# Expert gates scattered into DRAM, and expert products with 512-column records, in a float32 hybrid block kernel

## The chip, the cores and the metric

The program runs on one core of one Trainium2 chip. The metric is the device time of one execution in microseconds (us), as the median of several runs. A profiled execution gives the trace from which all rows below come.

## What is computed

The block takes 256 tokens of width 2048. After adaptive norms, a gated delta net and sparse attention, it ends with a layer of 128 x 128 = 16,384 experts (PEER), and this is the part that is changed:

```python
def tok_block(i):
    xb = lax.dynamic_slice_in_dim(ht, i * TB, TB, axis=0)              # 128 tokens
    qh = (xb @ wq).reshape(TB, PEER_HEADS, PEER_QDIM)                  # 8 heads
    s1 = jnp.einsum('thd,hkd->thk', qh[..., :half], keys1)             # 128 scores
    s2 = jnp.einsum('thd,hkd->thk', qh[..., half:], keys2)
    v1, i1 = lax.top_k(s1, 16)
    v2, i2 = lax.top_k(s2, 16)
    cand = (v1[..., :, None] + v2[..., None, :]).reshape(TB, PEER_HEADS, 256)
    cidx = (i1[..., :, None] * 128 + i2[..., None, :]).reshape(TB, PEER_HEADS, 256)
    sc, pos = lax.top_k(cand, 16)
    eidx = jnp.take_along_axis(cidx, pos, axis=-1)                     # 8 x 16 experts of a token
    gw = jax.nn.softmax(sc, axis=-1)
    act = jax.nn.gelu(jnp.einsum('td,thkd->thk', xb, u[eidx]))
    return jnp.einsum('thk,thkd->td', gw * act, v[eidx])
```

Each token has 128 gates (8 heads of 16 experts). The kernel does not gather `u` and `v` by token: it computes gelu(u x) of all experts for all tokens, multiplies by a matrix of gates that is zero where an expert was not chosen, and multiplies by all of `v`.

## The kernel before, in words

All products are made in float32 by splitting each operand into a high part of a reduced float32 (`whi`, `hi`) and the rest (`wlo`, `lo`). A product is three matmuls: high x high, high x low, low x high. `Stream` (line 446) loads the weights in pieces by SP into `raw` (4 tiles of 128 x 1024), and for each 512 columns ACT casts `whi` and DVE subtracts `wlo`; 4 such pairs are open at a time. Line 289 is the helper through which every instruction is recorded, so the trace names it for nearly all, and instructions are told apart by their tiles.

Small work runs as generators in `Background` (line 316): after each step of the main loop `bg.step()` lets each of up to 8 open tasks run to its next `yield`, whose value is the planner's time at which it goes on. The planner's times (`Times`, line 196) only set the order of the instructions, which is fixed when the program is built.

The stages that the change touches:
- **The block's first stages** (until about 1040 us): norm, projections, delta net, attention. After the first projection the tasks `pre_task` and others are put in. ACT casts, activates, and issues a few DMAs here.
- **Query stage**: `wq` makes the 16 half-queries; `route_task` follows behind on DVE: scores, top 16 of each half, top 16 of the sums, for each of the 8 heads. After the last head it works out, in pieces of 1024 columns, the indices `i` and `j` of each chosen expert and the softmax, transposes these to put tokens on columns, and splits the gates into three bf16 parts (`gs`).
- **u loop** (line 1875 on): 128 steps j; step j makes the products of expert group (all i, this j) with all 256 tokens, 16 k-tiles of 3 matmuls of 256 columns (`stat256`), then a gelu into column block j of the matrix `A` (`act_by`).
- **`gate_task`** (line 1854) runs beside the u loop, 64 times for 4 tokens each: DVE builds one-hot matrices `oi` (128 x 128 x 4) and `ow` (three gate parts x one-hot), PE multiplies them (12 bf16 matmuls of 128 columns) into a gate matrix of 128 i x 128 j per token, DVE multiplies that into the columns of `A` that exist already, and ACT copies it to those that do not.
- **v loop** (line 2020 on): two halves of 1024 output columns, each 128 steps j: `w_split(j)` splits `A` of step j into `wh` and `wl`, and 12 matmuls of 512 columns follow. In the first half `g2_task` runs beside it: 64 DVE products with `ada_t`, whose loads SP issues. At its end POOL (GpSimd) issues the loads for the last norm.

POOL issues DMAs of its own queue in order, SP those of the weights.

Of the kernel before, what the change touches and what calls it, by code (L numbers as in the profile page):

```python
# [18 lines left out]
T = 256  # L19
# [48 lines left out]
def _const_array():  # L68
# [13 lines left out]
    add("one", np.ones(128))  # L82
    add("ones", np.ones((128, 128)))
# [96 lines left out]
NPAIR = 3  # L180
WO = [(512 * j, 512) for j in range(4)]
# [224 lines left out]
def _build(nc, tc, A, out, stacks, dump, at, stop_at):  # L406
# [33 lines left out]
    bg = Background(times, 8, lambda: "first" in done and next(ada_gen, None), lambda: PACE2 if "o7" in done else PACE)  # L440
# [108 lines left out]
    crowd = dram.tile([1, D], F32, name="crowd")  # L549

# [1115 lines left out]
    h2h = [hp.tile([128, 4, T], F32R, name="ht") for _ in range(4)]  # L1666
    h2l = [hp.tile([128, 4, T], F32R, name="ht") for _ in range(4)]
# [15 lines left out]
    for k in range(17):  # L1683
        if k == 0:
            stream.advance(0)
        if k < 16:
            pk = pairs[k // 2][:, k % 2 * 256:k % 2 * 256 + 256]
            hi, lo = h2h[k // 4][:, k % 4, :], h2l[k // 4][:, k % 4, :]
            h32 = xp.tile([128, T], F32, name="h32b", bufs=2)
            act(hi, pk, AF.Identity, bias=mcol[:, 3, k:k + 1], scale=mcol[:, 4, k:k + 1])  # L1690
            V.tensor_scalar(h32, pk, mcol[:, 4, k:k + 1], mcol[:, 3, k:k + 1], op0=OP.mult, op1=OP.add)
            V.tensor_tensor(lo, h32, hi, OP.subtract)
            if k % 2 == 0 and len(pairs) < 8:
                pairs += h2_pairs([len(pairs)])
        if k:
            h, l = stream.get()
            hi, lo = h2h[(k - 1) // 4][:, (k - 1) % 4, :], h2l[(k - 1) // 4][:, (k - 1) % 4, :]
# [5 lines left out]
    for k in range(4):  # L1703
        dump(f"h2h{k}", h2h[k])
        dump(f"h2l{k}", h2l[k])
# [5 lines left out]
    sp = pool(st_A, "sp", side=RIGHT)  # L1711
    st_e = stack()
# [23 lines left out]
    eqs = [qs_[:, 1024 * i:1024 * i + 1024] for i in range(2)]  # L1736
# [9 lines left out]
    gate = tmp(256)  # L1746
    eidx = tmp(512).rearrange("p (w b n) -> p w b n", w=2, b=2)

    ij = [ep.tile([128, T], BF, name=f"ij{n}") for n in range(2)]
    gs = [ep.tile([128, T], BF, name=f"gs{n}") for n in range(3)]  # L1750
    iota4 = ep.tile([128, 128, 4], BF, name="iota4")
    V.tensor_copy(iota4, C("iota")[:, :, None].to_broadcast([128, 128, 4]))
# [9 lines left out]
    def route_task():  # L1762
# [24 lines left out]
        V.tensor_copy(iif, ii)  # L1787
        V.tensor_scalar(au, posu, 4, None, op0=OP.logical_shift_right)
        V.tensor_copy(af[:, 0], au)
        V.tensor_scalar(au, posu, 15, None, op0=OP.bitwise_and)  # L1790
        V.tensor_copy(af[:, 1], au)
        yield bg.now() + RPACE
        for tb in range(2):
            for w in range(2):
                for h0 in (0, 4):
                    hs_ = slice(h0, h0 + 4)
                    eq = eqs[w].rearrange("p (h s k) -> p h s k", h=4, s=16)
                    V.tensor_tensor(eq, af[:, w, tb, hs_, :, None].to_broadcast([128, 4, 16, 16]),
                                    C("iota")[:, None, None, 0:16].to_broadcast([128, 4, 16, 16]), OP.is_equal)
                    yield bg.now() + RPACE  # L1800
                    V.tensor_tensor(eq, eq, iif[:, tb, w, hs_, None, :].to_broadcast([128, 4, 16, 16]), OP.mult)
                    yield bg.now() + RPACE
                    V.tensor_reduce(eidx[:, w, tb, :].rearrange("p (h s) -> p h s", h=8)[:, hs_], eq, axis=AX.X,
                                    op=OP.add)
                    yield bg.now() + RPACE
        for tb in range(2):
            V.tensor_tensor(gw[:, tb], scv[:, tb], scv[:, tb, :, 0:1].to_broadcast([128, 8, 16]), OP.subtract)
        yield bg.now() + RPACE
        act(gw, gw, AF.Exp)
        yield bg.now() + RPACE  # L1810
        sm = vv[:, 0, 0, :, 0:2].rearrange("p h b -> p b h")
        V.tensor_reduce(sm, gw, axis=AX.X, op=OP.add)
        V.reciprocal(sm, sm)
        V.tensor_tensor(gw, gw, sm[:, :, :, None].to_broadcast([128, 2, 8, 16]), OP.mult)
        yield bg.now() + RPACE
        for dst, src in zip((*ij, gate), (eidx[:, 0], eidx[:, 1], gw.rearrange("p b h s -> p b (h s)"))):
            S.copy(dst, transpose_to(ps(), src, 2).rearrange("p b t -> p (b t)"))
            yield bg.now() + RPACE
        for n in range(3):
            V.tensor_copy(gs[n], gate)  # L1820
            if n < 2:
                V.tensor_tensor(gate, gate, gs[n], OP.subtract)
        done.add("gate")

    def stat256(p, h, l, k0, n):

        for k in range(n):
            kk = k0 + k
            w, wl_ = h[:, k * 128:(k + 1) * 128], l[:, k * 128:(k + 1) * 128]
            a, b = h2h[kk // 4][:, kk % 4, :], h2l[kk // 4][:, kk % 4, :]  # L1830
# [19 lines left out]


    j_there, t_there = 0, 0

    def gate_task():
        nonlocal t_there
        nt = 4
        yield from wait_for("gate")
        ones, sums = {}, {}
        start, steps = bg.now(), 0
        pace = ((128 - j_there) * 5.15 - GEND) / (4 * T / nt)  # L1860

        def pause():
            nonlocal steps
            steps += 1
            return start + steps * pace

        def make(t0):
            oi = ep.tile([128, 128, nt], BF, name="oi", bufs=2)
            ow = ep.tile([128, 3, 128, nt], BF, name="ow", bufs=2)
            over = lambda a: a[:, None, t0:t0 + nt].to_broadcast([128, 128, nt])  # L1870
            V.tensor_tensor(ow[:, 2], iota4, over(ij[1]), OP.is_equal)
            V.tensor_tensor(oi, iota4, over(ij[0]), OP.is_equal)
            yield -pause()
            for n in range(3):
                V.tensor_tensor(ow[:, n], ow[:, 2], over(gs[n]), OP.mult)
            ones[t0] = oi, ow

        def products(t0):
            oi, ow = ones.pop(t0)
            p = ps()  # L1880
            for t in range(nt):
                for n in range(3):
                    PE.matmul(p[:, 128 * t:128 * t + 128], oi[:, :, t], ow[:, n, :, t], start=n == 0, stop=n == 2)
            sums[t0] = p

        def put(t0):
            nonlocal t_there
            pv = sums.pop(t0).rearrange("p (t j) -> p j t", t=nt)
            for q, (a, b) in enumerate(((0, JA), (JA, 128))):
                m = min(max(j_there, a), b)  # L1890
                x = act_by[q][:, :, t0:t0 + nt]
                if m > a:
                    V.tensor_tensor(x[:, :m - a], x[:, :m - a], pv[:, a:m], OP.mult)
                if m < b:
                    S.copy(x[:, m - a:], pv[:, m:b])
            t_there = t0 + nt

        yield from make(0)
        yield pause()
        for t0 in range(0, T, nt):  # L1900
            if t0 + nt < T:
                yield from make(t0 + nt)
                yield -pause()
            if t0:
                put(t0 - nt)
            yield pause()
            products(t0)
            yield pause()
        put(T - nt)
        done.add("gates")  # L1910

    bg.add(gate_task())
    for j in range(128):
        if j == JA:
            need("gate")
        p = ps()
        for i in range(4):
            h, l = stream.get()
            stat256(p[:, :T], h, l, 4 * i, 4)
        a = at_j(j)  # L1920
        n = t_there
        if n:
            t = ep.tile([128, T], F32, name="aj", bufs=2)
            act(t[:, :n], p[:, :n], AF.Gelu_apprx_tanh)
            V.tensor_tensor(a[:, :n], a[:, :n], t[:, :n], OP.mult)
        if n < T:
            act(a[:, n:], p[:, n:T], AF.Gelu_apprx_tanh)
        j_there = j + 1
    need("gates")
# [5 lines left out]
    vp_ = lambda: hp.tile([128, 1024], F32, name="ht")  # L1935
    ssf = sp.tile([128, 2, 4], F32, name="ssf")
# [10 lines left out]
    def g2_task():  # L1947
# [16 lines left out]
    bg.add(g2_task())  # L1964

# [59 lines left out]
    V.memset(ssf, 0.0)  # L2025
    ws = [w_split(j) for j in range(AHEAD)]
# [49 lines left out]
```

## Time and profile before

| | us |
|---|---|
| median of 3 runs (lowest to highest) | 2703.28 (2698.82 to 2706.44) |
| the profiled execution's own time | 2697.54 |
| its span in the trace | 2695.8 |

The granted TensorE clock is 0.995 of full speed over the span. How to read the rows that follow further down: a line of groups gives the engine, the operation, output <- inputs by tile name, the shape and the count, then the busy time and the mean duration of one, then idle time of the engine before it. A line of a timeline gives start, duration, engine and operation. Matmuls overlap, so that a matmul's pace is the distance between starts and not its duration. A window's line gives the busy time of each engine, the granted clock, the share of the 16 DMA engines and GB/s.

### The profile page before, as it was taken

How to read it: one execution, taken by the hardware profiler on the slowest of the kernel's cores; microseconds unless marked ns; L12 is line 12 of the kernel's file. 1: busy time of each engine (PE TensorE's matmuls, PEld its weight loads, DVE VectorE, ACT ScalarE, POOL GpSimd, SP SyncE). 2: the span in 40 equal slices, each digit the busy share in tenths (PEclk: the TensorE clock that was granted, in tenths of full speed). 3: DMA queues.
4: the chain of work that ended last, by engine and by line, in shares of the span. 5: the costliest groups of instructions: out<-in, count | busy, mean ns of one | idle time of the engine just before them, and what ended most of it. 6: DMA issues, size and time to landing. Idle time of an engine off the chain costs nothing.

```text
span 2695.8 us, 46915 instructions
## 1 busy us (share of the span) xinstructions
PE 2648.1 (98%) x17004; PEld 2278.1 (85%) x17004; DVE 1958.4 (73%) x4378; ACT 1393.3 (52%) x2983; POOL 36.6 (1%) x83
## 2 busy tenths in 40 slices
PE   8999999999999999999999999999999999999998
PEld 5777777777877778999999999999988888788886
DVE  6667877767777777999866666677577777766666
ACT  4446756565555445454544444444455555555555
POOL 0001000000000000000000000000000000000000
PEclk9999999999999999999999999999999999999999
DMA  9886756666676885555544444444577777765554
GB/s 348 310 313 229 243 174 199 197 225 229 226 241 234 291 311 200 177 173 187 185 160 152 155 157 157 153 157 155 179 256 235 235 234 235 251 193 189 188 188 157
DMA packets 176921, 571.15 MB, mean 212 GB/s; under 512 B 20048, under 2 KB 20384, under 8 KB 176176
## 3 DMA queue, kind: packets, MB, share of 16 engines
q1 hardware_dynamic: 168336, 538.21, 60.5%
q0 software_dynamic: 6624, 23.65, 2.5%
q10 hardware_dynamic: 1728, 6.29, 0.6%
q8 instruction: 133, 2.18, 0.3%
q14 instruction: 100, 0.82, 0.1%
HBM read 554.94 MB, written 13.13 MB: 211 GB/s over the span
## 4 chain that ended last, share of the span: by engine, by line
PE 91%; DVE 4%; ACT 2%; DMA 2%; issue 1%; ACTq 0%; DVEq 0%; POOLq 0%
PE ps L289 91%; DVE wlo L289 1%; DMA adas<-ada_t 1%; ACT whi L289 1%; DVE adas L289 0%; DMA raw<-w_in 0%; DVE cv L289 0%; ACT L289 0%; DVE ht L289 0%; DMA ccom<-consts 0%; DVE x L289 0%; ACT gsq L289 0%; DVE big L289 0%; ACT mix L289 0%; ACT o L289 0%
## 5 line engine op out<-in xcount | busy, mean ns | idle before, releaser
L289 DVE TENSOR_TENSOR wlo<-raw,whi 128x512 fp32r<-128x512 f32 (+2 forms) x1632 | 1098.2, 685 | 509.6 <-ACT whi L289 476.9
L289 ACT CAST whi<-raw 128x512 fp32r<-128x512 f32 (+2 forms) x1632 | 994.4, 618 | 772.7 <-PE ps L289 600.6
L289 PE MATMUL ps<-ht,whi 128*128 128x256 f32 x4608 | 828.8, 282 | 0.8 <-DVE ht L289 0.8
L289 PEld LDWEIGHTS ps<-ht,whi 128*128 128x128 f32 x4608 | 708.1, 189 | 1.2 <-DVE ht L289 1.0
L289 PE MATMUL ps<-ht,wlo 128*128 128x256 f32 x2304 | 647.2, 281 | 0.0
L289 PE MATMUL ps<-whi,ht 128*128 128x512 f32 (+2 forms) x1536 | 523.0, 403 | 5.0 <-ACT whi L289 3.8
L289 PEld LDWEIGHTS ps<-ht,wlo 128*128 128x128 f32 x2304 | 434.1, 188 | 0.0
L289 PE MATMUL ps<-wlo,wh 128*128 128x512 f32 x1024 | 408.6, 399 | 0.0
L289 PE MATMUL ps<-whi,wh 128*128 128x512 f32 x1024 | 403.7, 394 | 0.8 <-ACT wh L289 0.8
L289 PE MATMUL ps<-whi,wl 128*128 128x512 f32 x1024 | 401.5, 392 | 0.0
L289 PEld LDWEIGHTS ps<-whi,ht 128*128 128x128 f32 x1536 | 289.6, 190 | 87.3 <-issue 10.8
L289 PE MATMUL ps<-wlo,ht 128*128 128x512 f32 (+2 forms) x768 | 300.8, 392 | 3.4 <-DVE wlo L289 3.0
L289 PEld LDWEIGHTS ps<-whi,wh 128*128 128x128 f32 x1024 | 192.2, 188 | 50.8 <-ACT wh L289 1.0
L289 PEld LDWEIGHTS ps<-whi,wl 128*128 128x128 f32 x1024 | 192.2, 188 | 46.3 <-DVE wl L289 0.2
L289 PEld LDWEIGHTS ps<-wlo,wh 128*128 128x128 f32 x1024 | 192.2, 188 | 44.0
L289 PEld LDWEIGHTS ps<-wlo,ht 128*128 128x128 f32 x768 | 146.5, 191 | 32.3 <-DVE wlo L289 8.2
L289 ACT CAST wh<-A 128x256 fp32r<-128x256 f32 x256 | 103.7, 406 | 134.4 <-PE ps L289 134.4
L289 DVE SCALAR_TENSOR_TENSOR adas<-adas,crow 128x512 f32<-128x512 f32 x192 | 131.6, 686 | 43.1 <-DMA adas<-ada_t 42.8
L289 DVE TENSOR_TENSOR wl<-A,wh 128x256 fp32r<-128x256 f32 x256 | 109.0, 427 | 65.7 <-ACT wh L289 65.4
L289 PE MATMUL ps<-ow,oi 128*128 128x128 bf16 x768 | 101.3, 296 | 0.0
L289 ACT COPY A<-ps 128x192 f32<-128x192 f32 (+16 forms) x124 | 34.4, 307 | 114.1 <-DVE A L289 93.3
L289 PEld LDWEIGHTS <-oi 128*128 128x128 bf16 x768 | 81.7, 118 | 3.8
(323 smaller groups left out, 2298.6 us busy)
## 6 DMA issues: line engine op xcount, KB each, us to landing
raw<-u SPq DMA_DIRECT2D x256, 512.0 KB, 3.5
raw<-v SPq DMA_DIRECT2D x256, 512.0 KB, 3.6
raw<-w_in SPq DMA_DIRECT2D x170, 512.0 KB, 4.4
adas<-ada_t SPq DMA_DIRECT2D x192, 256.0 KB, 3.6
raw<-ada_w SPq DMA_DIRECT2D x64, 512.0 KB, 6.5
raw<-wn SPq DMA_DIRECT2D x32, 512.0 KB, 4.9
raw<-wo SPq DMA_DIRECT2D x32, 512.0 KB, 4.9
raw<-wq SPq DMA_DIRECT2D x32, 512.0 KB, 3.5
```

Source lines behind the costliest of these rows:

```text
L289: r = f(*args, **kw)
```

## The change

1. Two DRAM matrices `gated` (one per 128 tokens; 128 i x 128 j x 128 tokens, float32) are added. `zero_task` fills them with zeros early in the program, in 64 DMAs of 256 KB that ACT issues.
2. `route_task` calls `settle` after every second head: indices, softmax, and for each of these 32 experts of a token the position `place` = (i * 128 + j) * 128 + token. POOL then issues an indirect DMA for each expert slot n and each half of the tokens: 128 gates, one per partition, are added to `gated` at 128 places. There are 128 x 2 of them.
3. `gate_task` goes, with its one-hot matrices, its 768 bf16 matmuls, its multiplications and copies.
4. The tiles of the normed input hold high and low parts of a k-tile side by side. From the step at which routing is through, `stat512` replaces `stat256`: high weights x (high, low) in one matmul of 512 columns, low weights x high in one of 256. ACT then copies the second half of the sum, DVE adds it, and the gelu follows one step later.
5. In the first half of the v loop `gates_load` (POOL) brings `gated` back for 2 steps j at a time, 3 such tiles ahead, and DVE multiplies it into `A` (`gate_mult`, 128 x 512).
6. `g2_task` never runs two of its steps closer than 2 us of the planner's time.

```diff
+ZPACE = 5.0
+NGT = 3
+NSET = 2
...
+    gated = [dram.tile([128, 128, 128], F32, name=f"gated{tb}") for tb in range(2)]
+
+    def zero_task():
+        zero = per.tile([128, 512], F32, name="zero")
+        V.memset(zero, 0.0)
+        for js in range(0, 128, 4):
+            for g in gated:
+                S.dma_start(g[:, js:js + 4].rearrange("i j t -> i (j t)"), zero)
+                yield bg.now() + ZPACE
...
     bg.add(pre_task())
+    bg.add(zero_task())
...
+    h2 = [hp.tile([128, 2, 2, T], F32R, name="ht") for _ in range(8)]
+    def h2_of(k):
+        return h2[k // 2][:, k % 2, 0], h2[k // 2][:, k % 2, 1], h2[k // 2][:, k % 2].rearrange("p n t -> p (n t)")
...
+    def gates_load(j):
+        g = sp.tile([128, 2, 2, 128], F32, name="gates2", bufs=NGT)
+        for tb in range(2):
+            G.dma_start(g[:, tb], gated[tb][:, j:j + 2])
+        gates_of.append(g)
...
+            if h % NSET == NSET - 1:
+                yield from settle(slice(h - NSET + 1, h + 1))
+                done.add(f"settled{h}")
+        done.add("gate")
...
+        i, j = eidx[:, 0, :, ns], eidx[:, 1, :, ns]
+        V.scalar_tensor_tensor(i, i, 128.0, j, op0=OP.mult, op1=OP.add)
+        V.tensor_scalar(i, i, 128.0, C("tcol"), op0=OP.mult, op1=OP.add)
+        V.tensor_copy(place[:, :, ns], i)
         yield bg.now() + RPACE
...
+        for n in range(ns.start, ns.stop):
+            for tb in range(2):
+                nc.gpsimd.indirect_dma_start(
+                    gated[tb].rearrange("i j (t o) -> (i j t) o", o=1),
+                    bass.IndirectOffsetOnAxis(ap=place[:, tb, n:n + 1], axis=0),
+                    gate[:, tb, n:n + 1], None, compute_op=OP.add)
+
+    def stat512(p, h, l, k0, n):
         for k in range(n):
             kk = k0 + k
             w, wl_ = h[:, k * 128:(k + 1) * 128], l[:, k * 128:(k + 1) * 128]
+            a, _, ab = h2_of(kk)
+            PE.matmul(p, w, ab, start=kk == 0, stop=False)
+            PE.matmul(p[:, :T], wl_, a, start=False, stop=kk == 15)
+            bg.step()
...
-    def gate_task():
...
-    bg.add(gate_task())
+    last_p = None
     for j in range(128):
         if j == JA:
             need("gate")
         p = ps()
+        wide = "gate" in done
         for i in range(4):
             h, l = stream.get()
-            stat256(p[:, :T], h, l, 4 * i, 4)
...
+            if wide:
+                stat512(p, h, l, 4 * i, 4)
+            else:
+                stat256(p[:, :T], h, l, 4 * i, 4)
+            if i == 0 and last_p is not None:
+                act(at_j(j - 1), last_p[:, :T], AF.Gelu_apprx_tanh)
+                last_p = None
+        if wide:
             t = ep.tile([128, T], F32, name="aj", bufs=2)
...
+            S.copy(t, p[:, T:])
+            V.tensor_tensor(p[:, :T], p[:, :T], t, OP.add)
+            last_p = p
...
+    for j in range(0, 2 * NGT, 2):
+        gates_load(j)
...
-            yield max(start + G2PACE * m, v or 0.0)
+            yield -max(start + G2PACE * m, bg.now() + 2.0, v or 0.0)
...
+    def gate_mult(j):
+        a = act_by[j >= JA][:, j - JA * (j >= JA):j - JA * (j >= JA) + 2, :].rearrange("p j (b t) -> p b j t", b=2)
+        V.tensor_tensor(a, a, gates_of[j // 2], OP.mult)
+        if j + 2 * NGT < 128:
+            gates_load(j + 2 * NGT)
...
+            if half == 0 and j % 2 and j + 3 < 128:
+                gate_mult(j + 3)
```

How the order of instructions changes at three places (`DMASW`, `DMAHW` and an engine's name in brackets are the semaphores that an instruction waits for; `DMASW` are those of POOL's own DMAs, 8 in turn).

PE inside the u loop, at the first batch of gate products before; `ht` are the parts of the input, `whi` and `wlo` the weights of u, `ow` and `oi` the one-hot matrices:

```order
L289 MATMUL ps_15191<-ht_11099,whi_15171 128x256 [waits Activation_49]
L289 MATMUL ps_15191<-ht_11103,whi_15171 128x256
L289 MATMUL ps_15191<-ht_11099,wlo_15172 128x256 [waits DVE_49]
L289 LDWEIGHTS oi_15090
L289 MATMUL ps_15235<-ow_15091,oi_15090 128x128
...
L289 MATMUL ps_15191<-ht_11099,whi_15171 128x256
L289 MATMUL ps_15191<-ht_11103,whi_15171 128x256
```

and a wide step of the changed kernel:

```order
L293 MATMUL ps_18708<-ht_11171,whi_18709 128x512 [waits Activation_49]
L293 MATMUL ps_18708<-ht_11171,wlo_18710 128x256 [waits DVE_49]
L293 MATMUL ps_18708<-ht_11171,whi_18709 128x512
L293 MATMUL ps_18708<-ht_11171,wlo_18710 128x256
L293 MATMUL ps_18708<-ht_11172,whi_18709 128x512
```

Three matmuls of 256 columns for a k-tile become one of 512 and one of 256, and the 12 pairs of weight load and product per batch (64 batches) are gone. Of the 2304 k-tiles of the query stage and the u loop 1456 are wide, which is the u loop from j = 37 on (91 x 16).

POOL in the changed kernel, the first scatters and, after the last one, the first loads of gates (before, nothing stands between `keys` and the loads for the last norm):

```order
L293 DMA A1_11586<-keys 128x2048 [waits DMASW2_49,DMASW3_49,DMASW1_49,DMASW4_49,DMASW0_49,DMASW5_49,DVE_49,DMASW6_49,PE_49,DMASW7_49,Activation_49,Pool_49]
L1851 DMA gated0_75<-gate_11589,place_11588 2097152x1 [waits DMAHW7_49,DMAHW4_49,DVE_49]
L1851 DMA gated1_76<-gate_11589,place_11588 2097152x1 [waits DMAHW7_49,DMAHW3_49]
L1851 DMA gated0_75<-gate_11589,place_11588 2097152x1 [waits DMASW1_49]
L1851 DMA gated1_76<-gate_11589,place_11588 2097152x1 [waits DMASW2_49]
...
L1851 DMA gated0_75<-gate_11589,place_11588 2097152x1 [waits DMASW5_49]
L1851 DMA gated1_76<-gate_11589,place_11588 2097152x1 [waits DMASW6_49]
L293 DMA gates2_20879<-gated0_75 128x256 [waits DMASW7_49]
L293 DMA gates2_20879<-gated1_76 128x256 [waits DMASW0_49]
L293 DMA gates2_20882<-gated0_75 128x256
```

The semaphores go round in eights, so that the third scatter waits for the first and the fourth for the second: each scatter into one matrix waits until the one before it into that matrix has landed. The loads of gates wait for the last scatter. On DVE the position `place` of the first two heads is ready 25 weight pieces (`wlo`) after the last `MAX_INDEX` of head 1, and the first scatter waits for it.

DVE in the first half of the v loop, two steps j before:

```order
L289 TENSOR_TENSOR wlo_24050<-raw_23945,whi_24049 128x512 [waits Activation_49]
L289 TENSOR_TENSOR wlo_24062<-raw_23971,whi_24061 128x512 [waits DMAHW1_49,Activation_49]
L289 TENSOR_TENSOR wl_24072<-A0_11517,wh_24071 128x256 [waits PE_49,Activation_49]
L289 TENSOR_TENSOR wlo_24076<-raw_23971,whi_24075 128x512 [waits Activation_49]
L289 SCALAR_TENSOR_TENSOR ht_23458,ht_23459<-ht_23458,ht_23456 128x512 [waits DMAHW2_49]
L289 TENSOR_TENSOR wlo_24090<-raw_23999,whi_24089 128x512 [waits DMAHW3_49,Activation_49]
```

and in the changed kernel:

```order
L293 TENSOR_TENSOR wlo_21882<-raw_21787,whi_21881 128x512 [waits DMAHW0_49,Activation_49]
L293 SCALAR_TENSOR_TENSOR ht_20928,ht_20929<-ht_20928,ht_20926 128x512 [waits DMAHW1_49]
L293 TENSOR_TENSOR wl_21894<-A0_11585,wh_21893 128x256 [waits PE_49,Activation_49]
L293 TENSOR_TENSOR A0_11585<-A0_11585,gates2_21722 128x2x2x128 [waits DMASW2_49,DMASW1_49]
L293 TENSOR_TENSOR wlo_21902<-raw_21787,whi_21901 128x512 [waits Activation_49]
L293 TENSOR_TENSOR wlo_21914<-raw_21815,whi_21913 128x512 [waits DMAHW2_49,Activation_49]
```

One product of 128 x 512 with gates, which waits for POOL's loads, is added per two steps; the weight pieces behind it on DVE wait with it.

## Rows read from the trace of the kernel before

**Rows 1.** The page: busy time of the engines, and shares of the chain
```profile
PE 2648.1 (98%) x17004; PEld 2278.1 (85%) x17004; DVE 1958.4 (73%) x4378; ACT 1393.3 (52%) x2983; POOL 36.6 (1%) x83
...
PE 91%; DVE 4%; ACT 2%; DMA 2%; issue 1%; ACTq 0%; DVEq 0%; POOLq 0%
```

**Rows 2.** Windows: delta net and attention; u loop; v loop's halves
```profile
core 0: us, PE busy (x) PEld busy (x) DVE busy (x) ACT busy (x) POOL busy (x), PEclk, DMA share, GB/s
212.00:645.00 433.00, 416.88 (x2959) 324.44 (x2959) 327.58 (x919) 268.77 (x656) 5.10 (x14) 0.98 0.64 211
1143.00:1966.00 823.00, 823.00 (x6957) 819.04 (x6956) 590.22 (x1311) 376.75 (x830) 2.10 (x4) 1.00 0.52 165
1967.00:2322.00 355.00, 354.94 (x1521) 285.45 (x1522) 267.88 (x508) 197.17 (x383) 0.00 (x0) 1.00 0.73 240
2327.00:2685.00 358.00, 358.00 (x1536) 288.00 (x1536) 238.14 (x395) 200.70 (x394) 3.66 (x7) 1.00 0.60 190
```

**Rows 3.** Chain in order of time, from the query stage to the v loop
```profile
1045.57 920.74 PE ps L289 x7781
1966.31 0.02 issue
1966.33 0.05 ACT aj L289
1966.38 0.23 issue
1966.61 0.41 ACT wh L289
1967.02 0.04 issue
1967.06 1.01 PE ps L289 x3
```

**Rows 4.** Timeline of PE in the u loop (start, duration, count at the end)
```profile
1499.75 0.40 PE L289 MATMUL ps<-ht,whi 128*128 128x256 f32 x2
...
1506.73 0.27 PE L289 MATMUL ps<-ht,wlo 128*128 128x256 f32 x1
1506.85 1.58 PE L289 MATMUL ps<-ow,oi 128*128 128x128 bf16 x12
1508.17 0.49 PE L289 MATMUL ps<-ht,whi 128*128 128x256 f32 x2
```

**Rows 5.** Timeline of ACT: an ACT-issued DMA, and the idle time behind it
```profile
591.25 0.33 ACTq L289 DMA_DIRECT2D mixd<-mix  x1
591.62 1.14 ACT L289 CAST whi<-raw 128x512 fp32r<-128x512 f32 x2 [0.40 <-ACT mix L289]
```

**Rows 6.** Groups of DVE in the first half of the v loop
```profile
L289 DVE TENSOR_TENSOR wlo<-raw,whi 128x512 fp32r<-128x512 f32 x253 | 175.3, 693 | 53.7 <-ACT whi L289 40.2
L289 DVE TENSOR_TENSOR wl<-A,wh 128x256 fp32r<-128x256 f32 x129 | 54.9, 427 | 33.1 <-ACT wh L289 33.1
```

**Rows 7.** Page, DMA issues: count, KB each, median us from issue to landing
```profile
mix<-partd POOLq DMA_DIRECT2D x5, 512.0 KB, 4.9
x1d<-x POOLq DMA_DIRECT2D x8, 256.0 KB, 3.7
crowd<-crow POOLq DMA_DIRECT2D x1, 8.0 KB, 3.7
ht<-fnw POOLq DMA_DIRECT2D x2, 512.0 KB, 16.5
posi<-pos POOLq DMA_DIRECT2D x1, 1.0 KB, 5.9
modr<-ht POOLq DMA_DIRECT2D x1, 8.0 KB, 1.6
```

**Rows 8.** Groups of POOL: its DMA issues to DRAM
```profile
L289 POOL DMA_DIRECT2D x1d<-x x8 | 4.4, 552 | 87.3 <-DVE x L289 87.3
```

**Rows 9.** Timeline of DVE: the end of head 1's routing
```profile
1121.95 0.42 DVE L289 FIND_INDEX8 A<-A 128x8 uint32<-128x256 f32 x1
```

More of the change, by code (lines that the diff above doesn't have):

```diff
@@ L82, in _const_array @@
     add("one", np.ones(128))
+    add("tcol", t)
     add("ones", np.ones((128, 128)))
@@ L438, in acc2 @@
         return [ps(), ps()]
-    bg = Background(times, 8, lambda: "first" in done and next(ada_gen, None), lambda: PACE2 if "o7" in done else PACE)
+    bg = Background(times, 9, lambda: "first" in done and next(ada_gen, None), lambda: PACE2 if "o7" in done else PACE)
     done = set()
@@ L1711, in _build @@
     sp = pool(st_A, "sp", side=RIGHT)
+    gates_of = []
+    def gates_load(j):
[3 more added lines that the diff above has]
+        gates_of.append(g)
     st_e = stack()
@@ L1735, in _build @@
     qhs = [qs_[:, 256 * i:256 * i + 256] for i in range(16)]
-    eqs = [qs_[:, 1024 * i:1024 * i + 1024] for i in range(2)]
+    eqs = [qs_[:, NSET * 256 * i:NSET * 256 * (i + 1)] for i in range(2)]
     work = [[tmp(512) for _ in range(4)]]
@@ L1745, in _build @@
     gw = tmp(256).rearrange("p (b h s) -> p b h s", b=2, h=8)
-    gate = tmp(256)
     eidx = tmp(512).rearrange("p (w b n) -> p w b n", w=2, b=2)
[L1749 to L1752, printed above, removed]
+    place = ep.tile([128, 2, 128], U32, name="place")
+    gate = ep.tile([128, 2, 128], F32, name="gate")
     MIN = -3.0e38
@@ L1794, in route_task @@
             for w in range(2):
[L1795 to L1805, printed above, removed]
+                eq = eqs[w].rearrange("p (h s k) -> p h s k", h=NSET, s=16)
@@ new lines, in settle @@
+                V.tensor_tensor(eq, af[:, w, tb, hs_, :, None].to_broadcast([128, NSET, 16, 16]),
+                                C("iota")[:, None, None, 0:16].to_broadcast([128, NSET, 16, 16]), OP.is_equal)
+                V.tensor_tensor(eq, eq, iif[:, tb, w, hs_, None, :].to_broadcast([128, NSET, 16, 16]), OP.mult)
+                V.tensor_reduce(eidx[:, w, tb, :].rearrange("p (h s) -> p h s", h=8)[:, hs_], eq, axis=AX.X,
+                                op=OP.add)
+                yield bg.now() + RPACE
@@ L1812, in route_task @@
-        V.tensor_reduce(sm, gw, axis=AX.X, op=OP.add)
+        ns = slice(16 * hs_.start, 16 * hs_.stop)
+        sm = vv[:, 0, 0, hs_, 0:2].rearrange("p h b -> p b h")
+        V.tensor_reduce(sm, gw[:, :, hs_], axis=AX.X, op=OP.add)
         V.reciprocal(sm, sm)
-        V.tensor_tensor(gw, gw, sm[:, :, :, None].to_broadcast([128, 2, 8, 16]), OP.mult)
-        yield bg.now() + RPACE
-        for dst, src in zip((*ij, gate), (eidx[:, 0], eidx[:, 1], gw.rearrange("p b h s -> p b (h s)"))):
-            S.copy(dst, transpose_to(ps(), src, 2).rearrange("p b t -> p (b t)"))
-            yield bg.now() + RPACE
@@ L1819, in route_task @@
[L1819 to L1823, printed above, removed]
+        V.tensor_tensor(gate[:, :, ns].rearrange("p b (h s) -> p b h s", s=16), gw[:, :, hs_],
+                        sm[:, :, :, None].to_broadcast([128, 2, NSET, 16]), OP.mult)
+        i, j = eidx[:, 0, :, ns], eidx[:, 1, :, ns]
+        V.scalar_tensor_tensor(i, i, 128.0, j, op0=OP.mult, op1=OP.add)
+        V.tensor_scalar(i, i, 128.0, C("tcol"), op0=OP.mult, op1=OP.add)
@@ L1847, in _build @@
             done.add(f"qh{ct // 2}")
-    j_there, t_there = 0, 0
-    def gate_task():
[L1855 to L1910, printed above, removed]
-    bg.add(gate_task())
+    last_p = None
     for j in range(128):
@@ L2025, in _build @@
     V.memset(ssf, 0.0)
+    gate_mult(0)
+    gate_mult(2)
     ws = [w_split(j) for j in range(AHEAD)]
```

43 lines of the change are left out of this document (18 added, 25 removed).

## The prediction

> **What bounds the kernel now.** I read the page's busy shares and the chain of waits first. PE is busy for 2648.1 of 2695.8 us and holds 91% of the chain; no other engine is over 73% [rows 1]. So PE's instructions are the time, as long as the others keep up. Next I read the windows of the stages that are touched [rows 2]: in the u loop (1143 to 1966) PE has no idle time at the full granted clock, while DVE is busy 72%, ACT 46%, and DMA moves 165 GB/s. In the first half of the v loop PE is as full, but DVE is at 75% and DMA at 240 GB/s. Third comes the chain in order of time [rows 3]: PE alone from 1045.57 to 1966.31, then 0.75 us through ACT, and PE again. Whatever leaves PE between those two points ends the u loop earlier by the same amount.
>
> **The change, part by part.** The profiled execution took 2697.54 us, 5.7 below the median of 2703.28; the sum is made against the first and then carried to the second.
>
> *Gate products leave PE.* In the timeline 60 matmuls of 256 columns start between 1499.75 and 1506.85, so one costs 118.3 ns; a batch of 12 gate matmuls takes from 1506.85 to 1508.17, 1.32 us [rows 4]. There are 64 batches on an engine without idle time: **-84.5**. Six transposes go as well; at a twelfth of a batch each they make -0.7, and I write **-1**. DVE's and ACT's share of `gate_task` goes from engines with idle time: 0.
>
> *Wide records.* A k-tile costs 3 x 118.3 = 354.9 ns now. A 512-column matmul is taken from the v loop's second half, where 1536 of them fill 358.00 us: 233.1 ns [rows 2]. The new k-tile is 233.1 + 118.3 = 351.4 ns, 3.5 ns less, over 1456 k-tiles: **-5.1**. Merging two matmuls into one removes almost no time: columns are what PE is paid for. DVE and ACT get one add and one copy per step in place of the gate work, and the gelu is a step late, so PE waits for neither. The loop is then shorter, and the same weights need about 165 x 823 / 732 = 185 GB/s, below the 240 that the v loop shows.
>
> *From u to v.* The last step now passes a copy on ACT, an add (0.43, as `wl` [rows 6]) and a gate product (0.69, as `wlo`) on DVE before `wh` can be made, with handovers of 0.23 as in [rows 3]: **+2**.
>
> *Zeros.* ACT issues 64 DMAs. Behind one, ACT is idle for 0.40 us [rows 5], together 25.6 us. In 212 to 645 ACT is 62% busy and PE idle for 16 of 433 us [rows 2]; PE waits there for split weights now and then, so a part can show. Bounds 0 and 25.6; since ACT has 164 us free and the issues are spread, I take a quarter: **+6**. The bytes (16.8 MB) add 39 to 211 GB/s, a share of 0.64 going to 0.76, about the 0.73 at which a v half keeps PE full [rows 2], so 0.
>
> *First half of v.* DVE gets 64 products of 128 x 512. At 0.69 each [rows 6] that is 44.3 us, which takes DVE from 267.9 to 312 of 355 us, 88%. The gates add 16.8 MB, 47 to 240 GB/s, a share of 0.73 going to 0.87. The nearest rows are the waits of DVE on ACT, 40.2 + 33.1 = 73.3 us [rows 6]: if these stay, DVE has only 14 us to spare and 30 show; if they shrink, nothing shows, since they are waits of an engine that had time. They are mostly that: **+2**, ends 0 and 30.
>
> *POOL's tail.* The loads for the last norm, 16.5 us to landing [rows 7], stand in POOL's queue ahead of the last 6 loads of gates. Tiles are asked for 6 steps of 2.8 us ahead, 16.8 us, so the margin is about nil: **+3**, ends 0 and 5.
>
> *Scatters.* POOL now issues 256 of them; every second one waits for the landing of the one two before. Their chain starts when `place` of the first two heads is ready: head 1's last index ends at 1122.4 [rows 9], and 25 weight pieces of 4 k-tiles (1.42 us) later it is about 1158. It must end, with a load of gates of about 5 us behind it (`mix`, 512 KB, 4.9 [rows 7]), when the u loop ends: 1966.3 - 84.5 - 1 - 5.1 is 1876. That leaves 713 us for 128 pairs, **5.57 us per pair**. No row shows a scatter that adds. From below: 1.6, a small quiet transfer, and two issues of 0.55 [rows 7, 8]. Within the rows it ends at 5.9, a load of 1 KB of positions, 128 pieces of 8 bytes, which in size is closest to a scatter's 128 of 4 [rows 7]. The nearest in direction is `x1d<-x`, a write from SBUF to DRAM issued by POOL, 3.7; an add also reads first, for which I put 0.6, so **4.3**; between the ends I follow the direction and not the size, as 8 KB and 256 KB of writes took the same 3.7. The chain then ends at 1708, 168 us early: **0**. The cover is one u loop; if it goes, the price is 128 us for every us over 5.57.
>
> A rule speaks against this. The rows show POOL's issues at 0.55 us each in stretches in which DVE works [rows 8], with no wait for DVE to be seen. The Trainium skill ("SBUF — State Buffer", section "SBUF: two separate sides") says that DVE and GpSimd share a pair of ports by an exclusive lock, which a DVE operation with two SBUF inputs takes against a GpSimd operation that reads SBUF, and a two-port one against the writing of descriptors. By the row the pair costs 4.3 us; by the rule more, which is rival 2 below.
>
> *Sum*: -84.5 - 1 - 5.1 + 2 + 6 + 2 + 3 = -77.6, or 2619.9 against 2697.54; with the 5.7 to the median **2625**.
>
> **Rivals.**
>
> 1. *The scatters end last.* PE then waits at the start of the v loop for gates, where today it waits 0.75 us. The time is 2625 + 128 x (pair - 5.57): even with before at a pair of 6.18, slower from there; at 7 us 2808. For it: the 5.9 of the load in small pieces lies over the threshold, 128 separate 4-byte adds are in no row, and the DMA engines carry weights beside them. Against it: `crowd`, 8 KB, and `x1d`, 256 KB, both writes, took 3.7 alike [rows 7]. Chance 0.24: 0.03 below 6.1 us, 0.02 about even, 0.19 slower.
>
> 2. *POOL waits for DVE.* If each issue waited for one `wlo` of 0.69 [rows 6], a pair would grow by 1.38 to 5.68, 0.11 over the threshold: 14 us, **2639**. No wait of POOL on DVE is seen in the 0.55 [rows 8], which has no indirect DMA in it: chance 0.04.
>
> 3. *Thin covers.* All 25.6 us of ACT's issues reach PE (20 more), and half of DVE's 30 in the v half: 2625 + 20 + 15 = **2660**. For it: in 212 to 645 PE has already some waits [rows 2]. Against it: ACT has 38% free. Chance 0.10.
>
> 4. *A wide matmul costs only its columns.* The 512-column matmuls of the v loop take 233.1 ns; if that is a price of that loop and a wide one costs 512 columns at 2.4 GHz, 213.3, the 1456 k-tiles give 28.8 more: **2596**. Against it: PE is full in the u loop, and 118.3 for 256 columns stands over 106.7 by the same tenth. Chance 0.04. The Trainium skill ("TensorE: Matmul & The Clock Gate", section "Wait — 56ns, not 53.3ns?") gives 215.7 ns between starts at 512 columns; by that the time would be about 2600, and the trace's 233.1 disagrees.
>
> **How the numbers follow.** The forecast, everything hidden but the terms above, has 0.58, at 2605 to 2645 by the ends of its terms. A measurement of this kernel tells about 0.3% (8 us). Faster: 0.58 + 0.04 + 0.10 + 0.04 + 0.03 = 0.79; same 0.02; slower 0.19. The range, 2598 to 2730, takes in the forecast, rivals 2 and 3, half of rival 4, and rival 1 up to a pair of 6.39 us; about 0.17 is left out, nearly all above.
>
> **What would show it.** In the trace of the changed kernel: no tiles `ow` and `oi` on PE; a wide k-tile at 351 ns between starts, and the u loop about 90 us shorter; a pair of scatters every 4.3 us; the last scatter near 1710, and at the end of the u loop a gap of PE of 2 to 3 us. In 212 to 645 PE's idle time should be 16 plus 6, behind ACT's casts; in the first half of v DVE near 88% and PE idle for a few us, the last of it before the last gates. The prediction is wrong if the gap between the loops is tens of us with `gates2` ended by POOL's DMAs (rival 1), if idle time of PE in the early stages or the v half is over 20 us (rival 3), or if the wide k-tile is under 340 ns (rival 4).

## The result and the profile after

The changed kernel takes 2614.98 us (median of 4 runs, 2612.07 to 2625.61); the kernel before beside it 2702.89. The ratio is 0.9682, 95% interval 0.9651 to 0.9714: 88 us faster, where 78 were forecast, and inside the range. The profiled execution of the changed kernel took 2625.61 us (span 2623.8), the slowest of the four, that of the kernel before was among its fastest, so that the two traces differ by 72.0 us only.

The page of the changed kernel, busy time of the engines and shares of the chain, against [rows 1]:

```profile
PE 2561.7 (98%) x14774; PEld 2122.5 (81%) x14774; DVE 1873.9 (71%) x4089; ACT 1416.3 (54%) x2901; POOL 521.1 (20%) x467
...
PE 85%; DVE 6%; DMA 4%; ACT 3%; issue 1%; ACTq 0%; DVEq 0%; SPq 0%; POOLq 0%
```

PE stays the bound with 86 us less work. DMA rises from 2% to 4% of the chain. The windows of the same four stages show what changed in each (columns as in [rows 2]: span, busy time of each engine, granted clock, DMA share, GB/s):

```profile
212.00:655.00 443.00, 422.01 (x2982) 326.76 (x2982) 329.89 (x932) 274.09 (x665) 7.87 (x25) 0.98 0.73 246
1156.00:1886.00 730.00, 729.71 (x4727) 661.14 (x4726) 481.63 (x985) 398.09 (x746) 419.43 (x262) 1.00 0.68 186
1887.00:2243.00 356.00, 350.83 (x1487) 281.04 (x1488) 288.00 (x569) 193.40 (x376) 70.86 (x133) 0.99 0.84 289
2248.00:2606.00 358.00, 358.00 (x1536) 288.01 (x1535) 237.41 (x394) 201.56 (x394) 0.00 (x0) 1.00 0.54 185
```

In the u loop PE is full as before. PE is idle for 21 us in the early stage (16 before), and the first half of the v loop has 5 us in which PE is idle; DVE is at 81% there and DMA at 289 GB/s. The chain in order of time (start, duration, what) places those 5 us:

```profile
1058.49 155.02 PE ps L293 x1311
...
1355.99 530.10 PE ps L293 x3042
1886.11 0.38 ACT aj L293
...
1887.47 0.68 DVE A L293
1888.15 1.01 DVE wl L293 x3
...
1890.27 8.83 DMA ht<-ada_t
...
1899.92 5.30 DMA ht<-ada_t
...
1906.05 4.60 DMA ht<-ada_t
...
1912.97 417.04 PE ps L293 x1780
```

The query stage and the u loop run from 1058.49 to 1886.1, 827.6 us against 920.7 [rows 3]. Then, for 25 us, the chain goes through loads of `ada_t`, which did not stand on it before. The two traces by landmarks of PE's timeline:

| stretch, us | before | after | difference | forecast |
|---|---|---|---|---|
| start to the first column of `adas` | 19.9 | 22.2 | +2.3 | 0 |
| from there to the query stage | 1025.7 | 1036.3 | +10.6 | +6 |
| query stage and u loop | 920.7 | 827.6 | -93.1 | -90.6 |
| end of the loop to the first product of v's second half (the 1537th) | 360.6 | 368.6 | +8.0 | +7 |
| the rest | 368.9 | 369.1 | +0.2 | 0 |
| span | 2695.8 | 2623.8 | -72.0 | -77.6 |

The fourth line agrees in size only; the experiments show that its cause is another one.

The scatters: POOL's group of them, and a stretch of POOL's timeline in the changed kernel (in brackets the idle time before, and what ended it).

```profile
L1851 POOL DMA_INDIRECT gated<-gate,place x256 | 416.1, 1625 | 294.8 <-DMA gated<-gate,place 177.0 <-DVE place L293 80.5 <-issue 33.5
```
```profile
1501.95 1.54 POOL L1851 DMA_INDIRECT gated<-gate,place  x1 [1.03 <-DMA gated<-gate,place]
1504.10 1.70 POOL L1851 DMA_INDIRECT gated<-gate,place  x1 [0.61 <-DMA gated<-gate,place]
1506.10 1.54 POOL L1851 DMA_INDIRECT gated<-gate,place  x1 [0.30 <-issue]
...
1796.62 0.60 POOL L293 DMA_DIRECT2D gates<-gated  x1 [1.08 <-DMA gated<-gate,place]
```

An issue takes 1.6 us of POOL, three times the 0.55 of [rows 8]; from the start of an issue to its landing it takes 4.3 us at the median. From 1165.1 to the first load of gates at 1796.6 the 128 pairs took 4.9 us each. The chain was over about 90 us before the u loop ended.

### The profile page after: what moved, and what is told of

Same layout as the page of the kernel before. It is cut to its first block, busy times and chain, and to the rows that moved or that the text cites. A ratio compares the mean times of both kernels' runs of the same rounds, so it can differ in the third digit from the quotient of the medians.

```text
span 2623.8 us, 42855 instructions
## 1 busy us (share of the span) xinstructions
PE 2561.7 (98%) x14774; PEld 2122.5 (81%) x14774; DVE 1873.9 (71%) x4089; ACT 1416.3 (54%) x2901; POOL 521.1 (20%) x467
## 4 chain that ended last, share of the span: by engine, by line
PE 85%; DVE 6%; DMA 4%; ACT 3%; issue 1%; ACTq 0%; DVEq 0%; SPq 0%; POOLq 0%
PE ps L293 85%; DVE wlo L293 2%; DMA adas<-ada_t 2%; DMA raw<-w_in 1%; ACT whi L293 1%; DMA ht<-ada_t 1%; DVE adas L293 1%; DVE cv L293 1%; ACT L293 0%; ACT o L293 0%; DVE A L293 0%; DVE ht L293 0%; DMA ccom<-consts 0%; ACT gsq L293 0%; DVE big L293 0%
## 5 line engine op out<-in xcount | busy, mean ns | idle before, releaser
L293 PE MATMUL ps<-ht,whi 128*128 128x256 f32 (+1 forms) x3152 | 817.6, 335 | 0.8 <-DVE ht L293 0.8
L293 PEld LDWEIGHTS ps<-ht,whi 128*128 128x128 f32 x3152 | 533.5, 188 | 68.7 <-DVE ht L293 1.0
L1851 POOL DMA_INDIRECT gated<-gate,place x256 | 416.1, 1625 | 294.8 <-DMA gated<-gate,place 177.0
L293 POOL DMA_DIRECT2D gates<-gated x128 | 68.4, 539 | 353.5 <-DVE A L293 340.7
L293 ACT COPY aj<-ps 128x256 f32<-128x256 f32 x91 | 33.9, 373 | 78.6 <-PE ps L293 78.6
```

The lines of the kernel that those rows point to most:

```text
L293: r = f(*args, **kw)
L1851: nc.gpsimd.indirect_dma_start(gated[tb].rearrange("i j (t o) -> (i j t) o", o=1), bass.IndirectOffsetOnAxis(ap=place[:, tb, n:n + 1], axi ...
```

## The experiments

**The changed kernel once more**, no edit.

> The changed kernel once more, as the base of the others on this chip. Theory and rivals alike: 2615 us, ratio to the kernel before 0.968. Its trace tells whether the 12.9 us by which the changed kernel was late at the end of the early stages (DVE's 544th weight piece at 1055.0 against 1042.1 us) belong to the kernel (again 10 to 13 us) or to the one execution (anything between 0 and 13).

2615.29 us, ratio 0.9679 (0.9666 to 0.9692). In its trace the way from the first `adas` to the query stage is 6.2 us longer than in the kernel before, not 10.6. Six of the traces have the same instructions on all engines in that stretch (the changed kernel twice, the three kernels with edits behind it in the u and v loops, and the one with more scatters): 10.6, 6.2, 9.5, 6.5, 2.7 and 3.7 us, mean 6.5. One trace does not give this term to better than some 4 us. The start, too, comes in two lengths, 19.2 to 20.2 us or 22.1 to 22.8, for the same code (seven of the fourteen traces each); its 2.3 us are not the change's.

**Edit 6 undone.**

```diff
-            yield -max(start + G2PACE * m, bg.now() + 2.0, v or 0.0)
+            yield max(start + G2PACE * m, v or 0.0)
```

> Edit 6 undone: the steps of the task that multiplies ada_t wait again for the planner's own due times, without the two-microsecond minimum. Theory: the 9 us that were lost between the loops (weight piece 1120 to 1152 went from -80.2 to -71.0) come from this task, whose products came every 2.1 us instead of every 5.6, and whose loads met the weights and the gates in a full DMA; so the loss goes to 2 us or less and the time to about 2607. Rival: the loads of gates alone fill the DMA there; then 2613 to 2617 and the loss stays.

2618.6 us, ratio 0.9682 (0.9664 to 0.9701): no gain, though the loss at the start of v went. The timeline of DVE of the changed kernel shows what edit 6 does there, the products with `ada_t`:

```profile
1899.19 0.69 DVE L293 SCALAR_TENSOR_TENSOR ht<-ht 128x512 f32<-128x512 f32 x1 [5.16 <-DMA ht<-ada_t]
...
1901.35 0.68 DVE L293 SCALAR_TENSOR_TENSOR ht<-ht 128x512 f32<-128x512 f32 x1
...
1905.32 0.69 DVE L293 SCALAR_TENSOR_TENSOR ht<-ht 128x512 f32<-128x512 f32 x1 [1.13 <-DMA ht<-ada_t]
...
1907.48 0.68 DVE L293 SCALAR_TENSOR_TENSOR ht<-ht 128x512 f32<-128x512 f32 x1
...
1910.67 0.69 DVE L293 SCALAR_TENSOR_TENSOR ht<-ht 128x512 f32<-128x512 f32 x1 [1.90 <-DMA ht<-ada_t]
```

and the first such products in the kernel before:

```profile
1977.19 0.69 DVE L289 SCALAR_TENSOR_TENSOR ht<-ht 128x512 f32<-128x512 f32 x1
...
1982.76 0.68 DVE L289 SCALAR_TENSOR_TENSOR ht<-ht 128x512 f32<-128x512 f32 x1
...
1988.36 0.68 DVE L289 SCALAR_TENSOR_TENSOR ht<-ht 128x512 f32<-128x512 f32 x1
```

Before, one came every 5.6 us and DVE waited for none; now the first ten come 2.2 to 4.7 us apart, and DVE stands at the loads, with the weight pieces behind them. The windows of the changed kernel have DMA full at that place. After PE's wait of 2.0 us for `wh` they also show a granted clock of 0.50 (1.2 GHz) for 3 us:

```profile
1890.00:1893.00 3.00, 3.00 (x9) 2.32 (x8) 1.29 (x3) 1.46 (x3) 2.06 (x4) 0.50 0.88 270
1896.00:1900.00 4.00, 2.51 (x11) 1.69 (x9) 0.81 (x3) 1.80 (x4) 0.00 (x0) 1.00 1.03 414
1900.00:1905.00 5.00, 4.45 (x19) 3.63 (x20) 4.18 (x9) 1.69 (x4) 1.07 (x2) 1.00 1.00 375
```

PE's waits (who waits, for whom: us in total, times, longest), first of the changed kernel from 1885 to 1935, then of the kernel with edit 6 undone between the halves of v (2235 to 2260):

```profile
PE ps L293 <- DVE wlo L293: 4.1, 3, 2.0
PE ps L293 <- ACT wh L293: 2.0, 1, 2.0
```
```profile
PE ps L293 <- DVE mcol L293: 5.5, 1, 5.5
```

With edit 6 undone the 4.1 us at `wlo` are gone (counted from the loop's end, the 200th product of v starts 1.7 us later than in the kernel before, in place of 9.2), but the last `ada_t` product comes too late and PE waits 5.5 us for `mcol` between the halves (1.1 before). Edit 6 trades one wait for another of the same size.

A full DMA alone is not the cause. It was as full in the kernel before (first line below, from 1970 to 1973) and with edit 6 undone (second line), and PE did not wait for `wlo` at the start of v in either. The third line is the first product with `ada_t` of the kernel with edit 6 undone:

```profile
1970.00:1973.00 3.00, 3.00 (x14) 2.43 (x13) 1.97 (x4) 1.75 (x4) 0.00 (x0) 1.00 1.04 419
```
```profile
1900.00:1905.00 5.00, 4.97 (x22) 3.67 (x20) 1.29 (x3) 1.35 (x3) 0.00 (x0) 1.00 1.03 410
```
```profile
1908.15 0.68 DVE L293 SCALAR_TENSOR_TENSOR ht<-ht 128x512 f32<-128x512 f32 x1
```

What differs is how long after its load a product stands on DVE. With edit 6 undone the first load takes 9.2 us to land (issued at 1889.85), and its product comes at 1908.15, 18.3 us after the issue; before, it took 5.9 and the product came after 7.9. In the changed kernel DVE is at the first product 3.8 us after the issue at 1890.27, and that load takes 8.8 us.

**Doubled zeros**, into a second matrix, order kept.

```diff
+    spare = [dram.tile([128, 128, 128], F32, name=f"spare{tb}") for tb in range(2)]
...
-            for g in gated:
+            for g, g_ in zip(gated, spare):
                 S.dma_start(g[:, js:js + 4].rearrange("i j t -> i (j t)"), zero)
+                nc.scalar.dma_start(g_[:, js:js + 4].rearrange("i j t -> i (j t)"), zero)
```

(`S` issues on ACT and tells the planner, `nc.scalar` issues on ACT and does not.)

> ACT issues 128 DMAs of zeros in place of 64, the added ones into a spare DRAM matrix that nobody reads; the order of PE and DVE is that of the changed kernel. Theory: issue and bytes of the zeros cost 5 to 10 us in the early stages, so twice of them cost as much again: 2620 to 2625. Rival 1: what the early stages lost is due to the other order of their instructions, which the planner chose once ACT had 64 more: 2613 to 2617. Rival 2: the loss is noise: 2613 to 2617 too, and the trace's early stages then differ between the two kernels of equal order.

2625.26 us, ratio 0.9721 (0.9707 to 0.9734), 10 us more than the changed kernel on the same chip; its early stages are 11.1 us longer than before. More zeros cost more time, within the forecast's ends (0 to 25.6). That all of the 6.5 us of the changed kernel are theirs is not shown: no kernel without zeros was run.

**Zeros that the planner does not count**, which restores the early order of PE and DVE.

```diff
-                S.dma_start(g[:, js:js + 4].rearrange("i j t -> i (j t)"), zero)
+                nc.scalar.dma_start(g[:, js:js + 4].rearrange("i j t -> i (j t)"), zero)
```

> The 64 DMAs of zeros stay on ACT but the planner does not count them, so that PE and DVE keep the order of the kernel before in the early stages. Theory (zeros themselves cost): about 2615, with the early stages late by 5 to 13 us. Rival (the order costs): 2603 to 2608, with the early stages late by under 4 us.

2617.69 us, 0.9684 (0.9671 to 0.9697). With the early order of the kernel before, the early stages are still 5.7 us longer in its trace: the changed order is not what costs. (That order is kept although up to 9 tasks may be open in the changed kernel and 8 before, a part of the change that its list leaves out.)

**All steps narrow**: `stat512` never used.

```diff
-        wide = "gate" in done
+        wide = False
...
-    act(at_j(127), last_p[:, :T], AF.Gelu_apprx_tanh)
```

> Edit 4 undone alone: all steps of the u loop make three matmuls of 256 columns, and the copy and the add go; gates still come through the DRAM matrix. Theory (columns are paid, a merged matmul saves 2 to 3.5 ns per k-tile): 3 to 5 us longer in the loop less 1 at its end, 2617 to 2620 against 2615. Rival 4 of the prediction (a wide matmul costs only its columns at full clock): it would have saved 33 us, and this kernel would take 2640 or more.

2618.02 us, 0.9690 (0.9677 to 0.9703); the intervals overlap with the changed kernel's. The trace resolves it, by the start of the query stage in the chain and PE's last product of u:

```profile
1051.37 155.06 PE ps L293 x1311
```
```profile
1881.41 0.27 PE L293 MATMUL ps<-ht,wlo 128*128 128x256 f32 x1
```

Query stage and u loop take 830.3 us in place of 827.6. The wide records are worth 2.7 us, and the gates' leaving, with the six transposes, the other 90.4 against 920.7. The pace of the wide records stands in the changed kernel's PE timeline, 0.35 us from one k-tile to the next:

```profile
1879.56 0.40 PE L293 MATMUL ps<-ht,whi 128*128 128x512 f32 x1
1879.80 0.28 PE L293 MATMUL ps<-ht,wlo 128*128 128x256 f32 x1
1879.92 0.39 PE L293 MATMUL ps<-ht,whi 128*128 128x512 f32 x1
...
1885.57 0.39 PE L293 MATMUL ps<-ht,whi 128*128 128x512 f32 x1
```

16 k-tiles from 1879.92 to 1885.57 are 353.1 ns each, against 354.9 of three narrow matmuls [rows 4].

**The kernel before with one of three gate parts**, everything else of `gate_task` kept.

```diff
-                for n in range(3):
-                    PE.matmul(p[:, 128 * t:128 * t + 128], oi[:, :, t], ow[:, n, :, t], start=n == 0, stop=n == 2)
+                PE.matmul(p[:, 128 * t:128 * t + 128], oi[:, :, t], ow[:, 0, :, t], start=True, stop=True)
```

> The kernel before with one of the three gate parts left in its gate product: 4 matmuls per batch in place of 12, all of DVE's one-hot work, products and copies kept (the gates are then bf16 parts only). Theory (PE's columns are the price of gate_task, its DVE and ACT work costs nothing): 64 x 8 matmuls of 0.11 us go, 57 us, 2647. Rival (DVE's one-hot matrices set the pace of the batches and would show once PE is lighter): 2665 to 2700.

2643.87 us, 0.9786 (0.9773 to 0.98). Its chain has the query stage and the u loop in one piece:

```profile
1046.52 860.13 PE ps L289 x7269
```

860.1 against 920.7: 512 matmuls less are 60.6 us less, 0.118 us each, though DVE did all its one-hot work. That is 91 us for all 768; with the 90.4 of the kernel with narrow steps, PE's matmuls were the whole price of the gates in this loop.

**Zeros from POOL.**

```diff
-                S.dma_start(g[:, js:js + 4].rearrange("i j t -> i (j t)"), zero)
+                G.dma_start(g[:, js:js + 4].rearrange("i j t -> i (j t)"), zero)
```

> POOL issues the 64 DMAs of zeros in place of ACT; the order of PE and DVE in the early stages is then that of the kernel before, as in the kernel whose zeros the planner did not count (2617.7). Theory (what the zeros cost is ACT's time behind each issue): 4 to 9 us less, 2607 to 2612. Rival (their 16.8 MB delay the weights' loads): 2615 to 2618.

2618.07 us, 0.9693 (0.968 to 0.9706): no gain, and the early stages are 4.9 us longer than before in its trace. Taking the issues off ACT does not help.

**Small extra DMAs on ACT, and large ones on POOL**, into a second matrix (`g_`, as with the doubled zeros), order kept in both.

```diff
                 S.dma_start(g[:, js:js + 4].rearrange("i j t -> i (j t)"), zero)
+                nc.scalar.dma_start(g_[:, js, 0:16], zero[:, 0:16])
```

> 64 more DMAs on ACT, each behind one of zeros, that write 8 KB instead of 256 KB into a spare DRAM matrix; the order of PE and DVE is that of the changed kernel. Theory A (ACT's time for the issue is what zeros cost): as with the doubled zeros, 2622 to 2627. Theory B (the bytes are what they cost): 2614 to 2618.

```diff
                 S.dma_start(g[:, js:js + 4].rearrange("i j t -> i (j t)"), zero)
+                nc.gpsimd.dma_start(g_[:, js:js + 4].rearrange("i j t -> i (j t)"), zero)
```

> 64 more DMAs of 256 KB of zeros into a spare DRAM matrix, issued by POOL, beside the 64 of ACT; the order of PE and DVE is that of the changed kernel. Theory A (ACT's issues cost): 2614 to 2618. Theory B (the bytes cost): 2622 to 2627.

2623.3 us (0.9707, 0.9694 to 0.972) and 2630.86 us (0.9722, 0.9701 to 0.9743), where the doubled zeros had 0.9721 and the changed kernel 0.9679. Neither theory holds alone: 64 issues on ACT with hardly a byte cost 0.0028 of 2701 us, 8 us; the bytes without ACT cost 0.0043, 12 us (three of its five runs took 2631 to 2633 us, two 2618 and 2621); and both together, the doubled zeros, no more than the bytes. In the landing times one sees the second stream, DMA issues of the kernel with the large ones on POOL (KB each, median us from issue to landing):

```profile
raw<-w_in SPq DMA_DIRECT2D x170, 512.0 KB, 5.2
gated<-zero ACTq DMA_DIRECT2D x64, 256.0 KB, 4.5
spare<-zero POOLq DMA_DIRECT2D x64, 256.0 KB, 9.1
```

against 4.9 for `w_in` in the changed kernel, but 4.9 with the doubled zeros too. How ACT's issues and the bytes share the cost stays open.

**48 pairs of scatters more.**

```diff
-        for n in range(ns.start, ns.stop):
+        for n in [*range(ns.start, ns.stop), *range(ns.start, ns.start + 12)]:
```

> Twelve of each 32 experts of a group are scattered twice, 48 pairs of scatters more on the chain (176 in place of 128); those gates count twice. Theory (rival 1 of the prediction as a mechanism: the chain is hidden until it passes the end of the u loop, then every us shows): at 4.95 us a pair the chain begins at 1165 and ends about 2036, 150 us behind the end of the u loop, so PE waits there and the time is 2755 to 2785. Rival (the pairs shorten when more are queued, or the loads of gates do not wait for all scatters): under 2700, with PE's gap between the loops under 80 us.

2726.86 us, ratio 1.0095 (1.0077 to 1.0114), of two runs: about 1% slower than the kernel before. PE's waits from 1880 to 2260, and POOL's groups while the u loop runs (1165 to 1880) and after it (1890 to 1986), and the end of the wait in the chain:

```profile
PE ps L293 <- ACT wh L293: 114.9, 1, 114.9
```
```profile
L1851 POOL DMA_INDIRECT gated<-gate,place x291 | 474.7, 1631 | 240.7 <-DMA gated<-gate,place 203.2 <-issue 34.9 <-DVE wlo L293 2.6
...
L1851 POOL DMA_INDIRECT gated<-gate,place x53 | 81.8, 1543 | 16.2 <-issue 15.9 <-DMA gated<-gate,place 0.3
```
```profile
1985.34 2.91 DMA gated<-gate,place
1988.54 2.36 DMA gates<-gated
1992.18 11.16 PE ps L293 x35
```

The mechanism of rival 1 is real: one wait of 114.9 us at the start of v, named for ACT, whose `wh` comes last, but ended by the last scatter through the gates. The time is 28 to 58 us under what was expected. With 4.9 us a pair throughout the chain would have ended about 2028; but once the u loop was over, a pair took 3.7 us, two issues of 1.54 + 0.30, and no scatter waited for the landing of another (0.3 us in all, against 203.2). It ended at 1988.

**ada_t steps 4 us apart.**

```diff
-            yield -max(start + G2PACE * m, bg.now() + 2.0, v or 0.0)
+            yield -max(start + G2PACE * m, bg.now() + 4.0, v or 0.0)
```

> The least distance of the ada_t steps goes from 2 to 4 us of the planner's time, the rest of edit 6 stays. Theory (at 2 us the loads of ada_t fill the DMA at the start of the v loop and cost 8 us there; with the planner's due times, 5.6 us apart, the task ended too late and cost 6 us between the halves): at 4 us neither shows, 2607 to 2611, with the loss at the loop's start under 3 us and none between the halves. Rival (any task that is slow enough at the start is too late at the end): 2614 to 2619.

2613.46 us, 0.9676 (0.966 to 0.9693). In the trace it does what was expected, PE's waits from 1878 to 1930 being

```profile
PE ps L293 <- ACT wh L293: 2.0, 1, 2.0
PE ps L293 <- DVE wlo L293: 1.6, 1, 1.6
```

with none between the halves; the 1536th product of v starts 362.3 us after the loop, 6 us sooner than in the changed kernel's first trace and 4 sooner than in its second. The runs do not separate it from the changed kernel (ratio 0.9676 against 0.9679).

**That and zeros at half the rate.**

```diff
-ZPACE = 5.0
+ZPACE = 10.0
...
-            yield -max(start + G2PACE * m, bg.now() + 2.0, v or 0.0)
+            yield -max(start + G2PACE * m, bg.now() + 4.0, v or 0.0)
```

> A candidate: the ada_t steps at least 4 us apart, and the zeros at half the rate (ZPACE 10 in place of 5), so that they reach into the attention stages. If zeros cost by collision with the weights' loads, half the rate costs less, 2605 to 2611; if by the piece, the same as with 4 us alone, 2611 to 2615.

2633.41 us, 0.9747 (0.9734 to 0.976): 18 us worse than the changed kernel. PE's waits over its whole span begin with

```profile
PE ps L293 <- DVE sb L293: 22.4, 1, 22.4
PE ps L293 <- DVE wlo L293: 8.1, 13, 2.4
```

At the end of attention the program lets all background tasks finish (`bg.drain()`). The zeros, ended by 650 us in the changed kernel, last to 887 here: 8 of them are issued in a row from 877 on, nine `ada_t` products follow one another on DVE from 883 to 900, each behind its load, and the next norm (`sb`) stands behind them. That the zeros left over brought the products to that place is read from the order and not tested. None of the candidates beats the changed kernel beyond its interval.

## Why the prediction was right, and where it was not

- *What bounds the kernel.* Right. All that left PE in the query stage and the u loop shortened them, and the two kept their 827.5 to 827.9 us in all kernels with wide steps, whatever happened before them.
- *Gate products, -84.5.* Right in kind and 6 us too small: by the kernel with one of three parts a matmul is worth 0.118 us, 91 for the 768. The batch read in [rows 4] is 1.32 us from its first start to the next product of u. What is missing stands in the row behind it: the first product of u after a batch takes 0.205 us to the next start in place of 0.118. Over all 64 batches of that trace the distance is 1.335 and this loss 0.087 on average, 1.42 us a batch or 91 in all.
- *Wide records, -5.1.* The sign and smallness were right; they give 2.7, as a wide k-tile takes 353 ns and not 351.4. Rival 4 falls. The Trainium skill ("TensorE: Matmul & The Clock Gate", section "Wait — 56ns, not 53.3ns?") gives 215.7 ns from start to start at 512 columns; the trace disagrees, with 353.1 - 118.3 = 235 here and 233 in the v loop.
- *Zeros, +6.* Mean of six traces 6.5: the size came out, the mechanism is not shown. ACT's time behind an issue was to cost it, but with the zeros issued by POOL the early stages are still 4.9 us longer. Added issues on ACT do cost, 8 us for 64. That the bytes would cost nothing, because a DMA share of 0.73 was harmless in the v loop, is wrong at least for 16.8 MB more of them, which cost 12 us from POOL.
- *From u to v, +2.* PE waits 1.97 us for `wh` where it waited 0.77: +1.2. In the first trace 3 us at half clock follow this wait, in the second they do not.
- *First half of v, +2, and POOL's tail, +3.* Neither shows: PE has no wait at the 64 gate products, and none at the end of that half. In their place stand 4 to 8 us at the start of v from edit 6 (the way to the 1536th product in seven traces, against that with edit 6 undone). It is the one edit to which the prediction gave no term. The list of the change tells it as a restriction, "never closer than 2 us"; the edit also drops the wait until, by the planner, the load that a step issues has landed. So the steps came closer than before, from 2.2 us on instead of 5.6, and a product stood on DVE before its load had landed, just when gates, v and `ada_t` fill the DMA. The total of this stretch agreed with the forecast by chance. DVE rose to 81% in that half and not to 88%: instructions that follow without a gap start 0.60 us apart where one lasts 0.69 (1886.87, 1887.47 and 1888.07 at the start of v), and the forecast added whole durations.
- *Scatters, 0.* Right that they hide, with some luck in the size: 4.3 us a pair was taken from the landing of `x1d` plus 0.6 for a read, with issues of 0.55; 4.9 was measured, with issues of 1.84 and a landing of 4.3. No run shows the 0.6: with the DMA else idle a scatter landed in 3.0 us, under the 3.7 of `x1d`. A pair stayed under the threshold of 5.57, and with 48 pairs more the chain outlasted the loop. Rival 1 did not come, but its margin was 0.6 us a pair, and 0.3 with narrow steps, where a pair took 5.2.
- *Rival 2, POOL waiting for DVE.* In the kernel with 48 pairs more an issue took 1.63 us while DVE worked and 1.54 while DVE stood still, so about 0.2 us of a pair, not 1.38. The exclusive lock of which the Trainium skill tells ("SBUF — State Buffer", section "SBUF: two separate sides") shows here no more than that.
- *Rival 3, thin covers.* Partly: the early stages lost some 6 us, where 26 were allowed; DVE's gate products in the v half cost PE nothing that shows.
- *The sum.* The ends written at its terms (0 to 25.6, 0 to 30, 0 to 5) give 2614 to 2675, and not the 2605 to 2645 of the text. The 5.7 us from the profiled execution to the median did not carry over: the profiled executions of the changed kernel, 2625.61 and 2620.06, lie above its medians of 2614.98 and 2615.29, where that of the kernel before lay below. The sum without them was 2619.9. So the miss of 10 us comes mostly from this step and from the gate products.

## What to carry to other kernels

Where PE is full, as in this u loop, columns are what is paid: 768 matmuls taken from it returned 91 us, all that they took there, and merging 1456 pairs of matmuls returned 2.7. A chain of dependent DMAs hidden behind a loop is free only up to the loop's end, so write its period times its length beside the loop's time, and expect the period under load to differ from that at rest. When a pacing rule is edited, read on the order of instructions how far apart its steps now come, how long after its load each product stands, and what else loads at that place.

## What the runs showed of the hardware that was not expected

- An indirect accumulating scatter of 128 values holds POOL for 1.54 us, against 0.55 for a plain DMA; from the start of the issue it lands in 3.0 us with the DMA else idle and in 4.3 beside 185 GB/s of weights. So POOL sets the pace at rest (3.7 us a pair), and landing under load (4.9).
- 64 DMAs of 8 KB added on ACT in the early stages cost 8 us; 64 of 256 KB added there cost 10 to 11.
- Six traces of the same instructions differ by up to 8 us in the early stages, and the start of the program is 3 us longer in seven of all fourteen traces.
- A first product of 256 columns behind 12 of 128 took 0.205 us to the next start in place of 0.118 (mean of the 64 batches).
